# The first norm's product with the input: from GpSimd and ScalarE to one VectorE operation per tile

## The chip, the cores and the metric

The kernel runs on one core of a Trainium2 chip. The metric is the time of one execution on the device, in microseconds, as the median of several runs. TensorE multiplies matrices into PSUM, VectorE and ScalarE do the element-wise work, GpSimd does some of it, and SyncE only issues transfers. The profile calls them PE, DVE, ACT, POOL and SP.

## What is computed

A decoder block on 512 tokens of width 1024: an RMS norm modulated by a conditioning vector c, two attention mixers side by side, a gated merge, a second modulated norm and a squared-ReLU MLP. The part that the change touches is the first line of it:

```python
mod = c @ w_ada[layer] + b_ada[layer]
sh_a, sc_a, gt_a, sh_m, sc_m, gt_m = jnp.split(mod, 6, axis=-1)

h = modulate(rmsnorm(x, g_mix[layer]), sh_a, sc_a)   # rmsnorm(x, g) * (1 + sc_a) + sh_a
z = h @ w_in[layer]
```

## The kernel before

Activations lie transposed: x is eight tiles x0 to x7 of 128 channels by 512 tokens. A product in fp32 accuracy is made of three matmuls: every operand is split in a rounded part and the rest (hh and hl for h, w_hi and w_lo for a weight), and TensorE multiplies hh by w_hi, hh by w_lo and hl by w_hi.

**The start** (L76 to L269) is written in the order in which it runs; behind it a scheduler orders the instructions by its own model of their costs. ScalarE squares the tiles of x, VectorE adds the squares (L144), TensorE sums them over the channels, and some small operations (L157 to L165) give 1/rms of each token, rstd. Transposes with the identity (L168) spread it over all partitions into a PSUM tile, `rb`. The loop of L233 then goes through the eight tiles k of x:

- Modulation. `ada_dot` (L100) loads 128 columns of w_ada, 512 KB, and makes their dot products with c in one VectorE operation (L107), whose second output is a column of `mod`. Two such columns belong to a tile, scale and shift. L114 makes `a_k`, the tile's scale times the norm's gain, and L118 `shc`, its shift. The dots are spread: tile k's loop body makes the columns of tile k+1, one of them ahead of hl (L260) and one behind it (L263). The columns' buffers are five, so the transfer of one waits until the dot five before it has run. SyncE issues all loads in the order of the program.
- h. For tile 0, VectorE makes x0 times a_k times rstd in one operation that reads `rb` from PSUM (L248), ScalarE adds the shift and rounds into hh (L249), and VectorE makes hl as (x0 + shift) - hh (L251). ScalarE then copies rstd into SBUF, `rstd_sb` (L253). For tiles 1 to 7, GpSimd multiplies x_k by `rstd_sb` (L255), ScalarE makes hh from it with scale a_k and shift (L256), and then the same again into x_k without rounding (L258); VectorE subtracts (L261).
- The tile's weights, 448 KB, are rounded by ScalarE (L246), and VectorE makes the rest, w_lo (L250, L257).
- TensorE adds the tile's share to seven PSUM tiles at once (L267): seven matmuls hh by w_hi, seven hh by w_lo, seven hl by w_hi.

VectorE, ScalarE, GpSimd and TensorE each work through their own row of instructions in order, and wait for the others where they read what those make. Behind the loop the next weights are split (L183, L184) and multiplied (L197 to L199), and the seven tiles are evacuated from PSUM. Some microseconds later the first head's attention scores are formed (L547 to L555), read by VectorE (L344) and mixed on TensorE with the products of the second value unit.

Of the kernel before, what the change touches and what calls it, by code (L numbers as in the profile page):

```python
# [12 lines left out]
AF = mybir.ActivationFunctionType  # L13
ALU = mybir.AluOpType
# [5 lines left out]
KT = D // P  # L20
# [26 lines left out]
def block_kernel(ctx: ExitStack, tc: tile.TileContext, d):  # L47
    nc = tc.nc
# [17 lines left out]
    def tmp(name):  # L66
        return sb.tile([P, S], F32, name=name, tag="tmp", bufs=NB["tmp"])

    def f(ap):
        return ap.bitcast(F32)  # L70


    def wtile(shape=(P, 1024)):
        return sb.tile(list(shape), F32, name="w_raw", tag="w_raw", bufs=NB["raw"])
# [7 lines left out]
    xt = [big_x(f"x{k}") for k in range(KT)]  # L82
# [17 lines left out]
    def ada_dot(col, early=False):  # L100
        if early:
            w = sb.tile([P, 1280], F32, name="w_ada", tag="p", bufs=NB["p"])[:, 0:D]
        else:
            w = wtile()
        nc.sync.dma_start(w, d["w_ada"][col])
        junk = sb.tile([P, D], BF16, name="junk", tag="pT", bufs=NB["pT"])
        nc.vector.scalar_tensor_tensor(junk, w, 1.0, cb, op0=ALU.mult, op1=ALU.mult,  # L107
                                       accum_out=mod[:, col:col + 1])
# [3 lines left out]
    def scale_col(out, col, k, g):  # L112

        nc.vector.scalar_tensor_tensor(out[:, k:k + 1], mod[:, col:col + 1], badd[:, (k if g == C_GMIX else 8 + k):(k if g == C_GMIX else 8 + k) + 1],  # L114
                                       cols[:, g + k:g + k + 1], op0=ALU.add, op1=ALU.mult)

    def bias_col(col, n=1, scale=None):
        nc.vector.tensor_tensor(modb[:, col:col + n], mod[:, col:col + n],  # L118
                                cols[:, C_BADA + col:C_BADA + col + n], op=ALU.add)
# [107 lines left out]
    rb = st0.rstd("m", "o")  # L227
# [4 lines left out]
    NW = NG0 * P  # L232
    for k in range(KT):  # L233
        scale_col(amix, 2 * k, k, C_GMIX)
        if k == 0:
            ada_dot(1, True)
        bias_col(2 * k + 1)
        raw = wtile()
        nc.sync.dma_start(raw[:, :NW], d["w_g0"][k])
        a_k = amix[:, k:k + 1]  # L240
        shc = modb[:, 2 * k + 1:2 * k + 2]
        hh = big_a(f"hh{k}", F32R)
        hl = big_a(f"hl{k}", F32R)
        whi = sb.tile([P, 1024], F32R, name="w_hi", tag="w_hi", bufs=NB["hi"])
        wlo = sb.tile([P, 1024], F32R, name="w_lo", tag="w_lo", bufs=NB["lo"])
        nc.scalar.activation(whi[:, :NW], raw[:, :NW], AF.Copy)  # L246
        if k == 0:
            nc.vector.scalar_tensor_tensor(xt[k], xt[k], a_k, rb, op0=ALU.mult, op1=ALU.mult)  # L248
            nc.scalar.activation(hh, xt[k], AF.Identity, bias=shc)  # L249
            nc.vector.tensor_tensor(wlo[:, :NW], raw[:, :NW], f(whi[:, :NW]), op=ALU.subtract)  # L250
            nc.vector.scalar_tensor_tensor(hl, xt[k], shc, f(hh), op0=ALU.add, op1=ALU.subtract)  # L251
            rstd_b = tmp("rstd_sb")
            nc.scalar.activation(rstd_b, rb, AF.Copy)  # L253
        else:
            nc.gpsimd.tensor_tensor(xt[k], xt[k], rstd_b, op=ALU.mult)  # L255
            nc.scalar.activation(hh, xt[k], AF.Identity, bias=shc, scale=a_k)  # L256
            nc.vector.tensor_tensor(wlo[:, :NW], raw[:, :NW], f(whi[:, :NW]), op=ALU.subtract)  # L257
            nc.scalar.activation(xt[k], xt[k], AF.Identity, bias=shc, scale=a_k)  # L258
            if k < KT - 1:
                ada_dot(2 * k + 2, True)  # L260
            nc.vector.tensor_tensor(hl, xt[k], f(hh), op=ALU.subtract)  # L261
        for c in range(2 * k + 2 if k == 0 else 2 * k + 3, min(2 * k + 4, 2 * KT)):
            ada_dot(c, True)  # L263
        h.append((hh, hl))
        for w, v in ((whi, hh), (wlo, hh), (whi, hl)):
            for n in range(NG0):
                nc.tensor.matmul(g0_ps[n], w[:, n * P:(n + 1) * P], v, start=(k == 0 and w is whi and v is hh),  # L267
                                 stop=(k == KT - 1 and v is hl))
# [430 lines left out]
    for step in ORDER.split():  # L699
        op, a = step[0], int(step[1:] or 0)  # L700
# [48 lines left out]
    xt = [big_x(f"xr{k}") for k in range(KT)]  # L749
# [48 lines left out]
    for hf, tok in enumerate(HALVES):  # L798
# [4 lines left out]
        rb = st1.rstd("m", "o", tok)  # L803
        for k in range(KT):
            shc = modb[:, SCM + 2 * k + 1:SCM + 2 * k + 2]
            hh, hl = h2[k][0][:, tok], h2[k][1][:, tok]
# [208 lines left out]
    for hf, tok in enumerate(HALVES):  # L1015
# [6 lines left out]
        rb = st2.rstd("m", "o", tok)  # L1022
        k = 0
# [120 lines left out]
```

## Time and profile before

| | us |
|---|---|
| median of 3 runs | 822.92 (822.32 to 823.15) |
| the profiled execution | 820.9 |
| its span, first to last instruction | 819.1 |

| engine | busy us | share of the span |
|---|---|---|
| PE (matmul) | 796.0 | 97% |
| DVE | 608.7 | 74% |
| ACT | 393.0 | 48% |
| POOL | 141.1 | 17% |

The profile shows one execution, about 2 us under the median of the timed runs. An engine's busy time is a mean over the whole span; what an edit of one stage is worth is read in that stage, from the waits of the engine that sets its end. In the timeline a row holds the start in us, the duration in us, the engine, the line, the operation, what it writes and reads, its size, the count, and in brackets the idle time before it with what ended that. Operations of one engine overlap a little at their ends, so the distance from one start to the next is somewhat shorter than a duration.

### The profile page before, as it was taken

To read this page: it belongs to the slowest core of one execution; us is meant where nothing else is said; L and a number is where in the kernel's file an instruction comes from. 1 tells how busy PE (TensorE), PEld (TensorE's weight loads), DVE (VectorE), ACT (ScalarE), POOL (GpSimd) and SP (SyncE) were. 2 spreads that over 40 slices of the span, in tenths; PEclk is the share of its full clock that TensorE was granted. 3 is DMA by queue.
4 is the path that set the end of the run, shared out by engine and by line. 5 is a ranking of instruction groups with operands and counts; after the bars stand their busy time and mean duration, and the time that the engine had idled before them with its cause. 6 is when DMAs were issued, how large, how long until landed. Compare 5 with 4: busy or idle time off the path is not lost.

```text
span 819.1 us, 11898 instructions
## 1 busy us (share of the span) xinstructions
PE 796.0 (97%) x4444; PEld 645.2 (79%) x4444; DVE 608.7 (74%) x1179; ACT 393.0 (48%) x742; POOL 141.1 (17%) x123
## 2 busy tenths in 40 slices
PE   6899999999999999999999999999999999999896
PEld 3687668665577565888889998899899988998895
DVE  6978668887667788866677749886768776877854
ACT  5458526475334444332242446644574456445741
POOL 2500000000000000001300004450435043614200
PEclk8999999999999999999999999999999999999998
DMA  9683261010052034885247302333222422332203
GB/s 350 248 271 127 68 216 52 27 51 27 26 177 80 1 103 137 263 300 200 93 154 255 117 10 94 105 105 126 78 98 97 138 81 78 104 129 83 99 1 103
DMA packets 31005, 99.76 MB, mean 122 GB/s; under 512 B 3522, under 2 KB 5762, under 8 KB 30947
## 3 DMA queue, kind: packets, MB, share of 16 engines
q1 hardware_dynamic: 30880, 98.89, 35.9%
q8 instruction: 35, 0.57, 0.3%
q14 instruction: 24, 0.19, 0.1%
q0 software_dynamic: 64, 0.11, 0.0%
q10 hardware_dynamic: 2, 0.00, 0.0%
HBM read 96.89 MB, written 2.10 MB: 121 GB/s over the span
## 4 chain that ended last, share of the span: by engine, by line
PE 83%; DVE 7%; ACT 3%; DMA 2%; issue 2%; POOL 2%; SPq 0%; DVEq 0%; POOLq 0%; ACTq 0%
PE ps_acc L197 12%; PE ps_acc L199 12%; PE ps_acc L198 12%; PE ps_s L874 8%; PE ps_t L874 6%; PE ps_t L391 4%; PE ps_o L572 4%; PE ps_s L197 3%; PE ps_s L198 3%; PE ps_s L199 3%; PE ps_s L644 2%; PE ps_o L657 2%; POOL wsum L845 2%; DMA w_raw<-in_w_fc_dram 1%; DVE junk L107 1%
## 5 line engine op out<-in xcount | busy, mean ns | idle before, releaser
L183 ACT ACTIVATE w_hi<-w_raw 128x1024 fp32r<-128x1024 f32 x76 | 80.5, 1060 | 131.1 <-PE ps_acc L198 47.5
L184 DVE TENSOR_TENSOR w_lo<-w_raw,w_hi 128x1024 fp32r<-128x1024 f32 x76 | 99.5, 1311 | 54.4 <-ACT w_hi L183 54.2
L346 ACT ACTIVATE p<-p,nm 128x128 f32<-128x128 f32 (+3 forms) x96 | 53.3, 556 | 59.1 <-DVE nm L344 57.8
L199 PE MATMUL ps_acc<-hh,w_lo 128*128 128x512 f32 x200 | 80.1, 401 | 0.0
L198 PE MATMUL ps_acc<-hl,w_hi 128*128 128x512 f32 x200 | 79.8, 399 | 0.0
L197 PE MATMUL ps_acc<-hh,w_hi 128*128 128x512 f32 x200 | 79.7, 399 | 0.0
L379 DVE COPY pT<-ps_t 128x512 f32<-128x512 f32 (+1 forms) x72 | 42.4, 599 | 28.1 <-PE ps_o L572 15.8
L832 ACT ACTIVATE ws_hi<-wsum 128x512 fp32r<-128x512 f32 x56 | 35.3, 631 | 57.7 <-POOL wsum L845 55.0
L107 DVE SCALAR_TENSOR_TENSOR junk<-w_raw,cb 128x1024 bf16<-128x1024 f32 x32 | 38.5, 1220 | 17.9 <-DMA w_raw<-in_w_ada_dram 17.9
L845 POOL TENSOR_TENSOR wsum<-w_raw 128x512 f32<-128x512 f32 x28 | 39.2, 1399 | 65.1 <-DMA w_raw<-in_w_fc_dram 53.6
L845 POOL TENSOR_TENSOR wsum<-wsum,w_raw 128x512 f32<-128x512 f32 x28 | 45.9, 1640 | 25.2 <-DVE ws_lo L833 24.9
L198 PEld LDWEIGHTS ps_acc<-hl,w_hi 128*128 128x128 f32 x200 | 37.6, 188 | 10.8 <-issue 4.2
L197 PEld LDWEIGHTS ps_acc<-hh,w_hi 128*128 128x128 f32 x200 | 37.6, 188 | 10.8 <-issue 3.9
L199 PEld LDWEIGHTS ps_acc<-hh,w_lo 128*128 128x128 f32 x200 | 37.6, 188 | 10.5 <-issue 3.8
L833 DVE TENSOR_TENSOR ws_lo<-wsum,ws_hi 128x512 fp32r<-128x512 f32 x56 | 42.9, 796 | 3.1 <-PE ps_t L874 1.8
L197 PE MATMUL ps_acc<-h2h,w_hi 128*128 128x512 f32 x112 | 43.6, 389 | 0.0
L198 PE MATMUL ps_acc<-h2l,w_hi 128*128 128x512 f32 x112 | 43.6, 389 | 0.0
L199 PE MATMUL ps_acc<-h2h,w_lo 128*128 128x512 f32 x112 | 43.6, 389 | 0.0
L874 PE MATMUL ps_t<-t,ws_hi 128*128 128x256 f32 x224 | 40.5, 281 | 0.7 <-DVE t L962 0.4
L391 PEld LDWEIGHTS ps_t<-ident,p 128*128 128x128 f32 x240 | 27.6, 141 | 16.1 <-issue 5.4
L833 DVE TENSOR_TENSOR w_lo<-w_raw,w_hi 128x1024 fp32r<-128x1024 f32 (+1 forms) x28 | 31.1, 1111 | 10.2 <-ACT w_hi L832 10.2
L391 PE MATMUL ps_t<-ident,p 128*128 128x128 f32 x240 | 37.2, 279 | 0.0
(528 smaller groups left out, 2275.5 us busy)
## 6 DMA issues: line engine op xcount, KB each, us to landing
w_raw<-in_w_fc_dram SPq DMA_DIRECT2D x64, 512.0 KB, 3.3
w_raw<-in_w_ada_dram SPq DMA_DIRECT2D x32, 512.0 KB, 4.3
w_raw<-in_w_z_dram SPq DMA_DIRECT2D x25, 512.0 KB, 4.3
w_ada<-in_w_ada_dram SPq DMA_DIRECT2D x16, 512.0 KB, 6.5
w_raw<-in_w_c_dram SPq DMA_DIRECT2D x8, 512.0 KB, 4.2
w_raw<-in_w_o_dram SPq DMA_DIRECT2D x8, 512.0 KB, 4.6
w_raw<-in_w_out_dram SPq DMA_DIRECT2D x8, 512.0 KB, 3.2
w_raw<-in_w_g_dram SPq DMA_DIRECT2D x8, 448.0 KB, 7.0
```

The source lines that it names most:

```text
L107: nc.vector.scalar_tensor_tensor(junk, w, 1.0, cb, op0=ALU.mult, op1=ALU.mult, accum_out=mod[:, col:col + 1])
L183: nc.scalar.activation(hi[:, :n], raw[:, :n], AF.Copy)
L184: nc.vector.tensor_tensor(lo[:, :n], raw[:, :n], f(hi[:, :n]), op=ALU.subtract)
L197: nc.tensor.matmul(out, w[0], x[0], start=first, stop=False)
L198: nc.tensor.matmul(out, w[0], x[1], start=False, stop=False)
L199: nc.tensor.matmul(out, w[1], x[0], start=False, stop=last)
L346: nc.scalar.activation(o, o, AF.Exp, bias=nm, scale=-1.0, accum_out=sm)
L379: nc.vector.tensor_copy(dst, src)
L391: nc.tensor.transpose(pp[:, off:off + P], aps[i][:, kb * P:(kb + 1) * P], ident)
L833: nc.vector.tensor_tensor(lo, src, f(hi), op=ALU.subtract)
L845: nc.gpsimd.tensor_tensor(t, sums[x_] if isinstance(x_, int) else x_, y_, op=ALU.add)
L874: nc.tensor.matmul(out, w[a_][:, k], x[k][b_], start=(first and k == 0 and j == 0), stop=(k == 3 and j == 2), skip_group_check=True)
```

## The change

Tiles 1 to 7 get what tile 0 has. VectorE makes x_k times a_k times rstd in one operation that reads `rb` from PSUM, ScalarE makes hh with the shift as its bias, and VectorE makes hl from x_k, the shift and hh in one operation. GpSimd's products, ScalarE's second pass over x_k and the copy `rstd_sb` are gone. The dots stay spread as they were, and SyncE's transfers keep their order in the start.

```diff
         nc.scalar.activation(whi[:, :NW], raw[:, :NW], AF.Copy)
-        if k == 0:
-            nc.vector.scalar_tensor_tensor(xt[k], xt[k], a_k, rb, op0=ALU.mult, op1=ALU.mult)
-            nc.scalar.activation(hh, xt[k], AF.Identity, bias=shc)
-            nc.vector.tensor_tensor(wlo[:, :NW], raw[:, :NW], f(whi[:, :NW]), op=ALU.subtract)
-            nc.vector.scalar_tensor_tensor(hl, xt[k], shc, f(hh), op0=ALU.add, op1=ALU.subtract)
-            rstd_b = tmp("rstd_sb")
-            nc.scalar.activation(rstd_b, rb, AF.Copy)
-        else:
-            nc.gpsimd.tensor_tensor(xt[k], xt[k], rstd_b, op=ALU.mult)
-            nc.scalar.activation(hh, xt[k], AF.Identity, bias=shc, scale=a_k)
-            nc.vector.tensor_tensor(wlo[:, :NW], raw[:, :NW], f(whi[:, :NW]), op=ALU.subtract)
-            nc.scalar.activation(xt[k], xt[k], AF.Identity, bias=shc, scale=a_k)
-            if k < KT - 1:
-                ada_dot(2 * k + 2, True)
-            nc.vector.tensor_tensor(hl, xt[k], f(hh), op=ALU.subtract)
+        nc.vector.scalar_tensor_tensor(xt[k], xt[k], a_k, rb, op0=ALU.mult, op1=ALU.mult)
+        nc.scalar.activation(hh, xt[k], AF.Identity, bias=shc)
+        nc.vector.tensor_tensor(wlo[:, :NW], raw[:, :NW], f(whi[:, :NW]), op=ALU.subtract)
+        if 0 < k < KT - 1:
+            ada_dot(2 * k + 2, True)
+        nc.vector.scalar_tensor_tensor(hl, xt[k], shc, f(hh), op0=ALU.add, op1=ALU.subtract)
         for c in range(2 * k + 2 if k == 0 else 2 * k + 3, min(2 * k + 4, 2 * KT)):
             ada_dot(c, True)
```

In the new code the product stands in L247, hh in L248, w_lo in L249 and hl in L252; all lines behind the loop are nine lower.

VectorE's row in tile 1 (x_68 is x1; hh_213, hl_214 and hh_211, hl_212 are hh1 and hl1 before and after; junk is the dot's unused first output), as a piece of the difference:

```order
 L118 TENSOR_TENSOR modb<-mod,cols 128x1
-L257 TENSOR_TENSOR w_lo<-w_raw,w_hi 128x896
-L107 SCALAR_TENSOR_TENSOR junk,mod<-w_ada,cb 128x1024
-L261 TENSOR_TENSOR hl_214<-x_68,hh_213 128x512
+L247 SCALAR_TENSOR_TENSOR x_68<-x_68,amix,ps_o 128x512
+L249 TENSOR_TENSOR w_lo<-w_raw,w_hi 128x896
+L107 SCALAR_TENSOR_TENSOR junk,mod<-w_ada,cb 128x1024
+L252 SCALAR_TENSOR_TENSOR hl_212<-x_68,modb,hh_211 128x512
 L107 SCALAR_TENSOR_TENSOR junk,mod<-w_ada,cb 128x1024
 L114 SCALAR_TENSOR_TENSOR amix<-mod,badd,cols 128x1
```

One operation more per tile, in front of w_lo, and hl in the three-operand form; the dots and everything else keep their places.

TensorE's row some 10 us behind the loop, before (kh_509 and kl_511 are the keys' two parts, qst the query, zv the first value unit, hh_169, hh_213 and hh_256 are hh0, hh1 and hh2):

```order
L316 MATMUL ps_m<-ident,zg 128x32 x4
L197 MATMUL ps_acc<-hh_169,w_hi 128x512
L198 MATMUL ps_acc<-hl_170,w_hi 128x512
L199 MATMUL ps_acc<-hh_169,w_lo 128x512
L197 MATMUL ps_acc<-hh_213,w_hi 128x512
L554 MATMUL ps_s<-kh_509,qst 128x384
L555 MATMUL ps_s<-kl_511,qst 128x384
L198 MATMUL ps_acc<-hl_214,w_hi 128x512
L199 MATMUL ps_acc<-hh_213,w_lo 128x512
```

The same place now (kh_500, kl_502 the keys, hh_211 and hl_212 are hh1 and hl1):

```order
L197 MATMUL ps_acc<-hh_169,w_hi 128x512
L198 MATMUL ps_acc<-hl_170,w_hi 128x512
L307 MATMUL ps_m<-ident,zg 128x32 x4
L199 MATMUL ps_acc<-hh_169,w_lo 128x512
L197 MATMUL ps_acc<-hh_211,w_hi 128x512
L198 MATMUL ps_acc<-hl_212,w_hi 128x512
L199 MATMUL ps_acc<-hh_211,w_lo 128x512
L545 MATMUL ps_s<-kh_500,qst 128x384
L546 MATMUL ps_s<-kl_502,qst 128x384
```

The small transposes of the gates stand two matmuls later and the scores of 384 keys two matmuls later. The following 40 or so matmuls differ in the same manner, and VectorE's and ScalarE's rows there by the operations that belong to these scores; from the end of that stretch on the rows are the same again.

## Rows read from the trace of the kernel before

**Rows 1.** Waits of PE, 17 to 92 us: engine, line, waited-for: us, times, longest.

```profile
PE ps_acc L267 <- DVE hl L261: 1.5, 1, 1.5
PE ps_acc L267 <- ACT hh L256: 1.4, 1, 1.4
```

**Rows 2.** Busy time by stretch: us, PE, PEld, DVE, ACT, POOL, clock, DMA.

```profile
13.00:16.80 3.80, 1.11 (x4) 0.71 (x4) 3.52 (x11) 1.73 (x4) 0.00 (x0) 0.50 1.03 412
...
24.50:33.00 8.50, 5.52 (x24) 3.92 (x23) 8.50 (x10) 2.51 (x4) 6.75 (x9) 1.00 0.46 155
33.00:61.60 28.60, 28.60 (x127) 23.66 (x128) 23.53 (x43) 16.43 (x21) 0.00 (x0) 1.00 0.85 281
...
72.00:92.00 20.00, 19.54 (x90) 14.49 (x90) 18.75 (x65) 15.46 (x44) 0.00 (x0) 1.00 0.13 47
```

**Rows 3.** Timeline of PE, 24 to 62 us: first matmuls of tiles, waits, L197.

```profile
24.63 0.62 PE L267 MATMUL ps_acc<-hh,w_hi 128*128 128x512 f32 x2
...
29.51 0.74 PE L267 MATMUL ps_acc<-hl,w_hi 128*128 128x512 f32 x2 [1.54 <-DVE hl L261]
...
32.86 0.73 PE L267 MATMUL ps_acc<-hh,w_hi 128*128 128x512 f32 x2 [1.44 <-ACT hh L256]
...
37.75 0.61 PE L267 MATMUL ps_acc<-hh,w_hi 128*128 128x512 f32 x2
...
61.55 0.39 PE L197 MATMUL ps_acc<-hh,w_hi 128*128 128x512 f32 x1
```

**Rows 4.** Timeline of DVE, 15 to 36 us.

```profile
15.36 0.74 DVE L248 SCALAR_TENSOR_TENSOR x<-x,amix,ps_o 128x512 f32<-128x512 f32 x1
16.02 1.08 DVE L250 TENSOR_TENSOR w_lo<-w_raw,w_hi 128x896 fp32r<-128x896 f32 x1
17.02 0.75 DVE L251 SCALAR_TENSOR_TENSOR hl<-x,modb,hh 128x512 fp32r<-128x512 f32 x1
17.68 2.31 DVE L107 SCALAR_TENSOR_TENSOR junk<-w_ada,cb 128x1024 bf16<-128x1024 f32 x1
...
22.14 1.23 DVE L114 SCALAR_TENSOR_TENSOR amix<-mod,badd,cols 128x1 f32<-128x1 f32 x1
...
23.36 2.19 DVE L257 TENSOR_TENSOR w_lo<-w_raw,w_hi 128x896 fp32r<-128x896 f32 x1
...
27.72 1.74 DVE L261 TENSOR_TENSOR hl<-x,hh 128x512 fp32r<-128x512 f32 x1
...
31.62 0.21 DVE L114 SCALAR_TENSOR_TENSOR amix<-mod,badd,cols 128x1 f32<-128x1 f32 x1
...
31.82 1.08 DVE L257 TENSOR_TENSOR w_lo<-w_raw,w_hi 128x896 fp32r<-128x896 f32 x1
32.82 1.22 DVE L107 SCALAR_TENSOR_TENSOR junk<-w_ada,cb 128x1024 bf16<-128x1024 f32 x1
...
33.96 0.69 DVE L261 TENSOR_TENSOR hl<-x,hh 128x512 fp32r<-128x512 f32 x1
34.57 1.22 DVE L107 SCALAR_TENSOR_TENSOR junk<-w_ada,cb 128x1024 bf16<-128x1024 f32 x1
...
35.71 0.22 DVE L114 SCALAR_TENSOR_TENSOR amix<-mod,badd,cols 128x1 f32<-128x1 f32 x1
```

**Rows 5.** Timeline of POOL, its products merged.

```profile
17.43 13.18 POOL L255 TENSOR_TENSOR x<-x,rstd_sb 128x512 f32<-128x512 f32 x7 [14.77 <-ACT rstd_sb L253]
```

**Rows 6.** Timeline of ACT: hh of tile 0 and of tile 2.

```profile
16.14 0.72 ACT L249 ACTIVATE hh<-x,modb 128x512 fp32r<-128x512 f32 x1 [2.07 <-DVE x L248]
...
31.99 0.81 ACT L256 ACTIVATE hh<-x,modb,amix 128x512 fp32r<-128x512 f32 x1 [5.95 <-DVE modb L118]
```

**Rows 7.** DVE groups by shape, 340 to 480 us: count, busy, mean ns, idle.

```profile
L765 DVE SCALAR_TENSOR_TENSOR yb<-tab,ps_s 128x512 f32<-128x512 f32 x8 | 5.5, 688 | 5.5 <-PE ps_s L199 5.5
```

**Rows 8.** Instructions on the tile w_ada: its transfers from issue to landing.

```profile
DMA to landing us min/median/max: 3.2/6.5/9.3
```

**Rows 9.** Timeline of DVE, 60 to 96 us: a group of scalings.

```profile
82.56 1.01 DVE L369 TENSOR_SCALAR p<-p,rc 128x128 f32<-128x128 f32 x3
```

## The prediction

> **What bounds the kernel now.** TensorE is busy 97% of the span, so I read its waits first. Behind its first matmuls two of them lie in the loop that the change edits, the first modulation and projection (L233 to L268): one for hl1, which L261 makes on VectorE, and one for hh2, which L256 makes on ScalarE [rows 1]. The stretches by time say the same: of 24.5 to 33.0 us TensorE is busy 5.52 of 8.50 us, and from 33.0 to 61.6 it has no idle time at all, at a granted clock of 1.00 in both [rows 2]. So what an edit of this loop is worth is what it takes from those two waits, and nothing else, as long as the operands of the later tiles still come in time.
>
> TensorE's starts give the exact size. Tile 1's first matmul starts at 24.63 us, right behind tile 0's last, tile 2's at 32.86, tile 3's at 37.75, and the first matmul behind the loop (L197) at 61.55 [rows 3]. Tiles 3 to 7 follow each other without a wait, so one tile costs (61.55 - 37.75) / 5 = 4.76 us. Seven tiles would be 33.32 us; from 24.63 to 61.55 are 36.92. The difference, **3.60 us**, is what both waits cost with the slow first matmuls behind them.
>
> Why the operands are late stands in VectorE's row of instructions. Up to 17.4 us its operations have their usual lengths: 0.74 for the product x0 with PSUM (L248), 1.08 for w_lo. From 17.68 on a dot takes 2.31 (four of them do), the one-column amix 1.23, w_lo 2.19, hl1 1.74; from 31.62 on the same forms take 1.22, 0.21, 1.08 and 0.69 [rows 4]. That is 4 + 1 + 1 + 1 = 7 operations, each longer by 1.0 to 1.1 us, and it is the stretch in which GpSimd makes its seven products x times rstd, 17.43 to 30.61 us [rows 5]. VectorE has no idle time there (8.50 of 8.50 in one of the stretches), so about 7 x 1.07 = 7.5 us of its queue are lost beside GpSimd.
>
> **The change part by part.** *Removed:* GpSimd's seven products (L255), ScalarE's copy of rstd and its seven second passes over x (L253, L258). ScalarE waits for VectorE's modb in front of the hh of these tiles, by 5.95 us for hh2 [rows 6]; its passes lie beside such waits and are worth nothing by themselves. Without GpSimd's products I take VectorE's operations of 17.68 to 31.62 at the lengths that they have outside.
>
> *Added on VectorE, per tile 1 to 7:* one product of x with a_k and rstd in PSUM (L247), and hl as a three-operand form (L252) in place of a subtraction. Both forms stand in tile 0: from start to start x0 takes 16.02 - 15.36 = 0.66 and hl0 17.68 - 17.02 = 0.66, where the subtraction takes 34.57 - 33.96 = 0.61 [rows 4]. Tile 0's product ran while TensorE did little (1.11 of 3.80 us [rows 2]); the price of a read of PSUM beside running matmuls is shown by the same form on 512 columns in L765, 0.688 us long, eight times [rows 7]. So it is no dearer there, and I keep 0.66. The period of a tile on VectorE was 35.71 - 31.62 = 4.09 us and becomes 4.09 + 0.66 + 0.05 = 4.80, and with about 0.03 for a product that starts only when amix is through, **4.83 us**, 0.07 above TensorE's 4.76. VectorE is now the slower of the two, and what covers that is its lead.
>
> *The lead.* hl0 starts at 17.02 as before and the first dot at 17.68. Two dots at 1.14 from start to start (33.96 - 32.82) [rows 4] end at 19.96; amix and modb take 31.82 - 31.62 = 0.20, so L247 for x1 starts at 20.16 and ends at 20.90. ScalarE's hh takes 0.72 with bias alone [rows 6], so hh1 is there at about 21.7, before TensorE wants it at 24.63. w_lo1 ends near 21.9. The dot and then hl1 follow: hl1 runs from 22.96 to 23.7; TensorE wants it after 14 of the tile's 21 matmuls, at 24.63 + 3.17 = 27.80. The wait for hl1 is gone. x2 starts at 20.16 + 4.83 = 24.99, hh2 is there at 26.5 and is wanted at 24.63 + 4.76 = 29.39: the wait for hh2 is gone with 2.9 us to spare. Each later tile eats 0.07, so hh7 (50.7 against 53.19) still has some 2.5 us. TensorE is late on nothing in the loop, and the loop ends at 61.55 - 3.60 = 57.95.
>
> *What else could be late next.* The dots now run earlier and ask for their columns of w_ada earlier. A transfer is issued when the dot five before it has freed its buffer; the shortest such time is that of tile 3's second dot, whose buffer is free when tile 1's first dot ends (22.96) and which runs at 33.3, 10.3 us later; the slowest transfer of these columns took 9.3 to land [rows 8]. Covered, by a microsecond at the least. GpSimd's small memsets move to the start of its row, where the other engines wait for x, and a configuration step in front of its first product moves to the y stage, where the product's result is not the next thing that TensorE reads; I take nothing for either. Behind the loop all operands of the next products (w_hi, w_lo, the evacuations) are released by the same loop's matmuls or by hl7 and move with it.
>
> *Moved by the scheduler.* Behind the loop the order of TensorE's row changes in one place, some 11 us after the loop's end: the score matmuls of the first head and the products of the second value unit interleave a matmul or two later or earlier (the TensorE rows in the section on the change). The work is the same. TensorE loses 0.46 of 20.00 us there now, and VectorE, which must read each score before its PSUM buffer is used again, is busy 18.75 of 20.00 [rows 2]. So the new order can win at most 0.46 and could lose something that the trace does not show. I take 0 and put 0.4 of gain and 1.0 of loss in the range, the loss as a little more than the longest operation that could newly stand ahead of a score there, a 1.01 us group of scalings that now precedes one [rows 9].
>
> **Sum.** -3.60 us on the path, 0 for the rest. The profiled execution took 820.9 us (span 819.1), so it would become 817.3. It stands 2.0 us under the median of the three runs, 822.92; I take the same difference off the median: **819.3 us**, -0.44%.
>
> [...] Tile 0's hl0 is the form that all tiles now get, with two fp32 sources in SBUF: 0.75 us against 0.69 for the subtraction [rows 4]. [...]
>
> **The rivals.**
> 1. *The gain is spent again in the new order behind the loop.* For it: VectorE is 94% busy there, and the order was laid out by a scheduler's own model. Against it: TensorE's loss there is small with almost the same order, and later stages have no wait that is tied to an absolute time. To bring the time within 0.2% of before (1.65 us; about what a measurement of this kernel can tell from no change) it must lose 2 us or more, two scores late by a microsecond each. Time: about 821.9, from 821.3 to 822.9.
> 2. *VectorE's long operations are not GpSimd's doing*, but come from the transfers, which are dense in that stretch too. Then the seven operations stay long and two products are added in front of hh2: it comes 2 x 0.68 later plus the wait for the product and its pass on ScalarE, near 34.8 instead of 32.8. TensorE then follows VectorE at 4.83 per tile: 34.8 + 5 x 4.83 + 4.76 = 63.7 instead of 61.55, **+2.2 us, 825.1**, slower. It decides as soon as hh7 comes later than 56.79, which is a period of 5.84 on VectorE from x1 at 20.16 on. Against it: from 13.0 to 16.8 us the transfers run at 412 GB/s and VectorE's operations have their short lengths, and from 24.5 to 33.0 they move only 155 GB/s and the operations are long [rows 2, 4].
> [...]
>
> **How the numbers follow.** The forecast, within about a microsecond of 819.3: 0.77. Rival 1: 0.12. Rival 2: 0.05. Rival 3: 0.03; the rest, 0.03, goes to costs that no row points at. Faster by over 0.2% are the forecast, rival 3 and 0.01 of the rest: 0.81. Same: rival 1 and 0.01: 0.13. Slower: rival 2 and 0.01: 0.06. The range: 0.4 us of gain and 1.0 of loss from the moved order, and the spread of the three runs (822.32 to 823.15) on either side, 818.0 to 821.1; to take in rival 3 with its spread and the lower edge of rival 1, it goes to 821.6. That leaves out most of rival 1 and rival 2, somewhat under 2 in 10.
>
> **What would show it.** In the changed kernel's trace: no wait of TensorE for hl or hh between 17 and 58 us; the first L197 about 3.6 us earlier, near 57.95; all sixteen dots near 1.22 us and w_lo near 1.08; L247 and L252 near 0.74; a tile's period on VectorE near 4.83; GpSimd without products before the y stage; and TensorE's idle time in the 20 us of scores behind the loop still under a microsecond. [...]

## The result and the profile after

| | median us | runs |
|---|---|---|
| before | 823.15 | 5 (822.32 to 824.96) |
| the changed kernel | **818.24** | 5 (817.83 to 819.28) |

The ratio is 0.9948, 95% interval 0.9936 to 0.9959: 4.3 us less, with 3.4 and 5.3 as its ends; the two medians of the table differ by 4.91. The forecast was 819.3, faster. The profiled execution took 819.3 us, its span is 817.5.

The waits of TensorE from 17 to 92 us, where [rows 1] had one for hl1 and one for hh2 (columns: engine, what it makes, line, what it waited for; us in all, times, longest):

```profile
PE ps_acc L258 <- ACT hh L248: 1.7, 1, 1.7
PE ps_m L299 <- PE ps_acc L197: 0.4, 1, 0.4
PE ps_m L307 <- DVE krs L301: 0.3, 1, 0.3
```

What is left in the loop is the wait for hh0, ahead of the very first matmul, which the kernel before has too (1.7). The stretches by time (us, then busy time of PE, PEld, DVE, ACT, POOL, clock, DMA), which answer to [rows 2]; the last one is the stretch of the first scores, which before lay from 72 to 92:

```profile
24.50:33.00 8.50, 8.50 (x39) 7.03 (x38) 8.50 (x17) 2.92 (x4) 0.00 (x0) 1.00 0.95 322
33.00:57.60 24.60, 24.60 (x110) 20.38 (x109) 22.21 (x39) 8.79 (x13) 0.00 (x0) 1.00 0.78 256
68.40:88.40 20.00, 19.43 (x89) 14.70 (x90) 18.68 (x65) 15.42 (x44) 0.00 (x0) 1.00 0.11 43
```

TensorE is busy 8.50 of 8.50 us where it was busy 5.52. In the scores it loses 0.57 instead of 0.46. The starts of tiles 0, 1, 2 and 7 and of the first L197, which answer to [rows 3]:

```profile
17.81 1.22 PE L258 MATMUL ps_acc<-hh,w_hi 128*128 128x512 f32 x2 [1.74 <-ACT hh L248]
...
24.30 0.62 PE L258 MATMUL ps_acc<-hh,w_hi 128*128 128x512 f32 x2
...
29.06 0.62 PE L258 MATMUL ps_acc<-hh,w_hi 128*128 128x512 f32 x2
...
52.86 0.62 PE L258 MATMUL ps_acc<-hh,w_hi 128*128 128x512 f32 x2
...
57.62 0.39 PE L197 MATMUL ps_acc<-hh,w_hi 128*128 128x512 f32 x1
```

From 24.30 to 57.62 are 33.32 us, seven times 4.76 to the hundredth; before it was 36.92. VectorE from 17 to 58 us by shape (count, busy us, mean ns, idle), which answers to [rows 4]:

```profile
L107 DVE SCALAR_TENSOR_TENSOR junk<-w_ada,cb 128x1024 bf16<-128x1024 f32 x14 | 17.0, 1218 | 0.0
L249 DVE TENSOR_TENSOR w_lo<-w_raw,w_hi 128x896 fp32r<-128x896 f32 x8 | 8.7, 1084 | 0.0
L252 DVE SCALAR_TENSOR_TENSOR hl<-x,modb,hh 128x512 fp32r<-128x512 f32 x8 | 6.0, 747 | 0.0
L247 DVE SCALAR_TENSOR_TENSOR x<-x,amix,ps_o 128x512 f32<-128x512 f32 x8 | 6.0, 746 | 0.0
```

No long dot is left (1.22 each), and both three-operand forms take 0.75. The period of a tile, from one amix to the next (20.88, 25.75, and so on to 50.09), with the last hh, hh7, on ScalarE in the second fence:

```profile
20.88 0.21 DVE L114 SCALAR_TENSOR_TENSOR amix<-mod,badd,cols 128x1 f32<-128x1 f32 x1
...
21.13 0.75 DVE L247 SCALAR_TENSOR_TENSOR x<-x,amix,ps_o 128x512 f32<-128x512 f32 x1
...
25.75 0.21 DVE L114 SCALAR_TENSOR_TENSOR amix<-mod,badd,cols 128x1 f32<-128x1 f32 x1
```

```profile
51.12 0.72 ACT L248 ACTIVATE hh<-x,modb 128x512 fp32r<-128x512 f32 x1 [3.30 <-DVE x L247]
```

That is 4.87 us per tile, and hh7 is ready at 51.84, 1.0 us before TensorE takes it at 52.86.

### The profile page after: what moved, and what is told of

Same layout as the page of the kernel before. It is cut to its first block, busy times and chain, and to the rows that moved or that the text cites. A ratio compares the mean times of both kernels' runs of the same rounds, so it can differ in the third digit from the quotient of the medians.

```text
span 817.5 us, 11881 instructions
## 1 busy us (share of the span) xinstructions
PE 795.0 (97%) x4444; PEld 645.4 (79%) x4444; DVE 605.3 (74%) x1186; ACT 385.7 (47%) x734; POOL 127.1 (16%) x116
## 4 chain that ended last, share of the span: by engine, by line
PE 81%; DVE 5%; DMA 5%; ACT 4%; issue 3%; POOL 2%; SPq 0%; DVEq 0%; POOLq 0%; ACTq 0%
PE ps_acc L197 10%; PE ps_acc L199 10%; PE ps_acc L198 10%; PE ps_s L865 8%; PE ps_t L865 7%; PE ps_t L382 4%; PE ps_o L563 4%; DMA w_raw<-in_w_fc_dram 3%; PE ps_s L197 2%; PE ps_s L198 2%; PE ps_s L199 2%; PE ps_s L635 2%; PE ps_o L648 2%; POOL wsum L836 1%; PE ps_acc L258 1%
## 5 line engine op out<-in xcount | busy, mean ns | idle before, releaser
L183 ACT ACTIVATE w_hi<-w_raw 128x1024 fp32r<-128x1024 f32 x76 | 80.3, 1059 | 129.0 <-PE ps_acc L198 47.9
L199 PE MATMUL ps_acc<-hh,w_lo 128*128 128x512 f32 x200 | 80.2, 401 | 0.0
L197 PE MATMUL ps_acc<-hh,w_hi 128*128 128x512 f32 x200 | 79.6, 398 | 0.0
L197 PEld LDWEIGHTS ps_acc<-hh,w_hi 128*128 128x128 f32 x200 | 37.6, 188 | 10.8 <-issue 3.9
L199 PEld LDWEIGHTS ps_acc<-hh,w_lo 128*128 128x128 f32 x200 | 37.6, 188 | 10.4 <-issue 3.8
L197 PE MATMUL ps_acc<-h2h,w_hi 128*128 128x512 f32 x112 | 43.6, 389 | 0.0
L199 PE MATMUL ps_acc<-h2h,w_lo 128*128 128x512 f32 x112 | 43.6, 389 | 0.0
```

What stands on the lines that cost most here:

```text
L183: nc.scalar.activation(hi[:, :n], raw[:, :n], AF.Copy)
L197: nc.tensor.matmul(out, w[0], x[0], start=first, stop=False)
L199: nc.tensor.matmul(out, w[1], x[0], start=False, stop=last)
```

## The experiments

The theory: VectorE's long operations were GpSimd's doing, in that both read SBUF; the gain is TensorE's two waits. The rivals: the transfers made them long; or the gain comes from the shorter code on GpSimd and ScalarE and not from VectorE's lengths. Every run stands beside runs of the kernel before on the same chip, and the expectations call the runs by number: e1 to e4 (e1_again, e2_pool_reads, e3_pool_memsets, e4_no_product) share a median of 822.56 us, e5 to e8 (e5_extra_product, e6_two_tiles, e7_warm, e8_pool_copies) 822.12, and e9 to e12 (e9_again, e10_warm, e11_before_warm, e12_half_products) 822.51. Below they stand in the order of the argument: e1, e2, e3, e8, e4, e6, e5, e7 and e9 to e12.

### The changed kernel again

> The changed kernel itself, once more, to see how much of the first result (4.9 us less by the medians) is the loop. Theory A (the loop's two waits, 3.6 us, and nothing else): 3 to 4 us less than the kernel before in the same rounds; the loop itself, from the first matmul of tile 1 to the first L197, takes 7 x 4.76 = 33.3 us, as in the first profile. Rival B (the changed order behind the loop, or something later, gains too): 4.5 us or more less, and in the profile the distance from the first L197 to the last matmul shorter than the 750.7 us of the kernel before.

818.20 us, ratio 0.9947 [0.9933, 0.9961]. The loop's ends in its profile:

```profile
24.06 0.62 PE L258 MATMUL ps_acc<-hh,w_hi 128*128 128x512 f32 x2
...
57.38 0.39 PE L197 MATMUL ps_acc<-hh,w_hi 128*128 128x512 f32 x1
```

Again 33.32 us. The 4.4 us by the time lie between theory A's 3 to 4 and rival B's 4.5 or more; rival B's other sign fails, for from the start of the first L197 to that of the last matmul are 751.6 us here (57.38 to 809.00) and 750.5 before (61.55 to 812.02). The result stands, and 0.8 us of it are not placed.

### GpSimd's reads put back, for nothing

```diff
+        if k == 0:
+            rstd_b, dm = tmp("rstd_sb"), tmp("dm")
+            nc.scalar.activation(rstd_b, rb, AF.Copy)
+        else:
+            nc.gpsimd.tensor_tensor(dm, rstd_b, rstd_b, op=ALU.mult)
```

> The changed kernel with seven products on GpSimd beside the loop again, of a copy of rstd with itself into a scratch tile that nothing reads, released at the same point as the old ones; what is computed is the same. Theory G (GpSimd's reading of SBUF holds VectorE up): seven VectorE operations of some 18 to 32 us are again 1.0 to 1.1 us longer, VectorE's queue is 7.5 us late, hh7 comes near 59 instead of 52 us, the loop ends about 6 us later than in the changed kernel, and the time is some 5.5 to 6.5 us above it, 1 to 2 us above the kernel before. Rival T (the transfers made the operations long, and GpSimd was only there at the same time): all VectorE operations keep their lengths and the time is that of the changed kernel.

822.51 us, ratio 1.0001 [0.9991, 1.0012]: the whole gain is gone, though nobody reads what GpSimd makes. VectorE's timeline beside these products:

```profile
18.89 2.06 DVE L107 SCALAR_TENSOR_TENSOR junk<-w_ada,cb 128x1024 bf16<-128x1024 f32 x1
...
22.86 0.98 DVE L114 SCALAR_TENSOR_TENSOR amix<-mod,badd,cols 128x1 f32<-128x1 f32 x1
23.77 0.15 DVE L118 TENSOR_TENSOR modb<-mod,cols 128x1 f32<-128x1 f32 x1
23.96 0.75 DVE L247 SCALAR_TENSOR_TENSOR x<-x,amix,ps_o 128x512 f32<-128x512 f32 x1
...
27.81 1.51 DVE L252 SCALAR_TENSOR_TENSOR hl<-x,modb,hh 128x512 fp32r<-128x512 f32 x1
```

Four dots of 2.05 to 2.06, the amix, one w_lo (1.27) and the hl are longer, by 5.1 us in all. The product of L247, which has one of its two tensor inputs in PSUM, keeps its 0.75 in the same stretch. So does modb its 0.15, although both its inputs are in SBUF; it stands right behind the amix. TensorE waits again, and once VectorE's lead is used up it follows VectorE's 4.87 per tile (33.04, 37.93, 42.81 in its starts):

```profile
25.52 0.74 PE L263 MATMUL ps_acc<-hh,w_hi 128*128 128x512 f32 x2 [0.41 <-ACT hh L248]
...
33.04 0.73 PE L263 MATMUL ps_acc<-hh,w_hi 128*128 128x512 f32 x2 [1.77 <-ACT hh L248]
```

I had expected 5.5 to 6.5 us of loss. It was 4.3, since a hold is at most 0.84 here and not 1.07 (5.1 us in all where I had put 7.5); the last experiment says why.

### GpSimd busy, but only writing

```diff
+        if k == 0:
+            rstd_b = tmp("rstd_sb")
+            nc.scalar.activation(rstd_b, rb, AF.Copy)
+        else:
+            for _ in range(4):
+                nc.gpsimd.memset(rstd_b, 0.0)
```

> The changed kernel with 28 memsets of 128x512 on GpSimd beside the loop, into the scratch copy of rstd: GpSimd writes SBUF for some 14 us from the same point on, but reads nothing; what is computed is the same. If VectorE is held up by GpSimd's reads alone: VectorE's operations keep 1.22, 1.08 and 0.74 us, time as the changed kernel. If any GpSimd access to SBUF holds it up: operations longer by up to half a microsecond each (a memset's length, 0.52), VectorE's period of 4.87 us per tile rises above 5.5 in that stretch, and the time goes up by 1 to 6 us.

817.59 us, ratio 0.9941 [0.9927, 0.9955]: no loss, with GpSimd busy in the same place for longer than its products were. GpSimd's timeline with all 28 memsets merged, and VectorE's dots by shape:

```profile
18.28 16.32 POOL L258 MEMSET rstd_sb<- 128x512 f32 x28 [15.63 <-ACT rstd_sb L255]
```

```profile
L107 DVE SCALAR_TENSOR_TENSOR junk<-w_ada,cb 128x1024 bf16<-128x1024 f32 x14 | 17.0, 1219 | 0.0
```

So it isn't that GpSimd works there, or writes SBUF there: a dot takes 1.22 beside the memsets and 2.06 beside the products of e2_pool_reads, which read SBUF. It is its reads.

### One input only

```diff
+        if k == 0:
+            rstd_b, dm = tmp("rstd_sb"), tmp("dm")
+            nc.scalar.activation(rstd_b, rb, AF.Copy)
+        else:
+            nc.gpsimd.tensor_copy(dm, rstd_b)
+            nc.gpsimd.tensor_copy(dm, rstd_b)
```

> The changed kernel with fourteen copies of rstd's tile into a scratch tile on GpSimd beside the loop (one input in SBUF each, where the old products had two); what is computed is the same. If any read of SBUF by GpSimd holds up VectorE's operations with two SBUF inputs: up to fourteen of them longer, each by about one copy's length (0.6 us or so), VectorE some 5 to 8 us late after them, time 3 to 5 us above the changed kernel. If only GpSimd's operations with two inputs do: lengths and time as in the changed kernel, 818.2.

821.87 us, ratio 0.9997 [0.9987, 1.0006]. A copy reads one tensor and takes 0.62 alone, and it holds VectorE up as well: dots of 1.63, an amix of 0.55, while L247 stays at 0.75:

```profile
18.71 1.63 DVE L107 SCALAR_TENSOR_TENSOR junk<-w_ada,cb 128x1024 bf16<-128x1024 f32 x1
...
21.82 0.55 DVE L114 SCALAR_TENSOR_TENSOR amix<-mod,badd,cols 128x1 f32<-128x1 f32 x1
...
22.48 0.75 DVE L247 SCALAR_TENSOR_TENSOR x<-x,amix,ps_o 128x512 f32<-128x512 f32 x1
```

Six dots, three amix, one w_lo and two hl are long, by 4.6 us together; two waits for hh take the gain back.

### The kernel before without GpSimd's products

```diff
         else:
-            nc.gpsimd.tensor_tensor(xt[k], xt[k], rstd_b, op=ALU.mult)
             nc.scalar.activation(hh, xt[k], AF.Identity, bias=shc, scale=a_k)
```

> The kernel before without GpSimd's seven products: x of tiles 1 to 7 is left without its factor rstd, everything else runs as before (ScalarE's two passes, the subtraction for hl). Theory G: the whole gain of the change is GpSimd's absence, so VectorE's operations are short, both waits of TensorE in the loop are gone, and the time is that of the changed kernel within 0.5 us. Rival C (the gain comes from the shorter chain: one VectorE product in place of GpSimd's product and a ScalarE pass): hh1 and hh2 still late, time within 1 us of the kernel before.

818.54 us, ratio 0.9946 [0.9932, 0.9959]: the gain of the change, with ScalarE's two passes and VectorE's subtraction as they were before. Its loop:

```profile
24.57 0.63 PE L266 MATMUL ps_acc<-hh,w_hi 128*128 128x512 f32 x2
...
57.90 0.39 PE L197 MATMUL ps_acc<-hh,w_hi 128*128 128x512 f32 x1
```

33.33 us, and VectorE's fourteen dots have a mean of 1218 ns. This kernel also leaves out hh's wait for GpSimd's products; the run with the reads put back had no such wait and lost the gain all the same, so the wait is not the cause. What the change wins is that GpSimd is out; VectorE's added work costs nothing, and ScalarE's saved passes bring nothing.

### Two tiles in the new form

L247, L248 and L252 for tiles 1 and 2, the old form behind them, which leaves GpSimd five products:

```diff
+        if k < 3:
+            nc.vector.scalar_tensor_tensor(xt[k], xt[k], a_k, rb, op0=ALU.mult, op1=ALU.mult)
...
+        else:
+            nc.gpsimd.tensor_tensor(xt[k], xt[k], rstd_b, op=ALU.mult)
```

> The kernel before with the new form in tiles 1 and 2 alone; tiles 3 to 7 keep GpSimd's product and ScalarE's second pass. GpSimd then makes five products beside tiles 0 to 2 instead of seven. Theory G: five VectorE operations between 17 and 28 us are 1.0 to 1.1 us longer, VectorE is some 5.3 us late when it makes x2, hh2 comes near 32 instead of 29.4 us, and TensorE loses about 2.6 of the 3.6 us again: time 821 to 822. Rival C (the late operands came from the long chain over GpSimd and ScalarE, and the first two tiles were the late ones): both waits gone, time as the changed kernel, 818.2.

820.77 us, ratio 0.9984 [0.9975, 0.9994], a little under the 821 to 822 of theory G. GpSimd's products end at 26.92, and VectorE's next operation with two SBUF inputs has its short length:

```profile
17.64 9.28 POOL L258 TENSOR_TENSOR x<-x,rstd_sb 128x512 f32<-128x512 f32 x5 [14.98 <-ACT rstd_sb L256]
```

```profile
25.69 2.32 DVE L107 SCALAR_TENSOR_TENSOR junk<-w_ada,cb 128x1024 bf16<-128x1024 f32 x1
...
27.93 0.74 DVE L253 SCALAR_TENSOR_TENSOR hl<-x,modb,hh 128x512 fp32r<-128x512 f32 x1
```

TensorE waits for hh1 and hh2, though both now come in the new form:

```profile
25.27 0.72 PE L270 MATMUL ps_acc<-hh,w_hi 128*128 128x512 f32 x2 [1.60 <-ACT hh L249]
...
31.54 0.72 PE L270 MATMUL ps_acc<-hh,w_hi 128*128 128x512 f32 x2 [0.93 <-ACT hh L249]
```

So rival C, the long chain, falls. TensorE's seven tiles take 34.98 (25.27 to 60.25), so 1.66 of the 3.60 us are lost again; I had put it at 2.6.

### A second product on VectorE

```diff
+        if k == 1:
+            dm = tmp("dm")
+        if k > 0:
+            nc.vector.scalar_tensor_tensor(dm, xt[k], a_k, rb, op0=ALU.mult, op1=ALU.mult)
         nc.vector.scalar_tensor_tensor(xt[k], xt[k], a_k, rb, op0=ALU.mult, op1=ALU.mult)
```

> The changed kernel with the product of tiles 1 to 7 made twice on VectorE, the first time into a scratch tile that nothing reads (0.66 us more per tile); what is computed is the same. It prices VectorE's lead. From the changed kernel's rows: hh1 0.66 later, near 23.35 us, then hh of tile k at 23.35 + 5.53 (k - 1); TensorE wants it at 24.30 + 4.76 (k - 1). Theory L (VectorE is 0.11 us per tile slower than TensorE now and lives on a lead of about 1.6 us at tile 1): TensorE waits some 0.8 us in front of each tile from tile 3 on, the loop ends 3.4 to 3.7 us later, time 821.5 to 822. Rival (VectorE has room to spare beside TensorE): no waits, time as the changed kernel, 818.2.

824.05 us, ratio 1.0021 [1.0008, 1.0033], some 2 us above what I expected. VectorE's period is 5.65 (4.87 and 0.78, since the second product starts 0.78 behind the first), and TensorE follows it, tile by tile, as soon as the lead is gone. The last tile brings 1.2 us more. TensorE's starts of tiles 4, 6 and 7 and of L197, then ScalarE at the last tile:

```profile
40.44 0.73 PE L262 MATMUL ps_acc<-hh,w_hi 128*128 128x512 f32 x2 [0.56 <-ACT hh L252]
...
51.75 0.74 PE L262 MATMUL ps_acc<-hh,w_hi 128*128 128x512 f32 x2 [0.60 <-ACT hh L252]
...
58.60 0.73 PE L262 MATMUL ps_acc<-hh,w_hi 128*128 128x512 f32 x2 [1.76 <-ACT hh L252]
...
63.50 0.39 PE L197 MATMUL ps_acc<-hh,w_hi 128*128 128x512 f32 x1
```

```profile
56.88 1.06 ACT L183 ACTIVATE w_hi<-w_raw 128x1024 fp32r<-128x1024 f32 x1 [3.40 <-PE ps_m L262]
57.84 0.71 ACT L252 ACTIVATE hh<-x,modb 128x512 fp32r<-128x512 f32 x1
```

x7 was ready at 56.59, but ScalarE had a rounding of the next stage's weights (L183) in front of hh7, which itself waited for TensorE's tile 6. In the changed kernel hh7 comes first. So a tile of 4.87 on VectorE is covered by the lead and one of 5.65 isn't. Even without L183 in front, hh7 would have come near 57.3, behind the 56.79 that the prediction's second rival gave as the point from which it is slower than before.

### More idle matmuls ahead of the loop

TensorE waits for rstd at a granted clock of 0.50 (13.0 to 16.8 us in the kernel before [rows 2]), and tile 0 begins at it: pairs of 1.05 to 1.22 us, where later ones take 0.62. Two more of the idle matmuls that keep it busy, and four between the sums and the loop:

```diff
-WARM = (0, 2)
+WARM = (0, 2, 4, 5)
...
-    rb = st0.rstd("m", "o")
+    rb = st0.rstd("m", "o", between=lambda: nc.tensor.matmul(warm, ones, xt[6], start=True, stop=True))
+    for _ in range(3):
+        nc.tensor.matmul(warm[:, 0:256], ones, xt[7][:, 0:256], start=True, stop=True)
```

> The changed kernel with more idle matmuls on TensorE ahead of the loop: two more tiles of x behind the two that are there, one between the sums of the squares and the transposes of rstd, three half ones behind the transposes, all into a PSUM tile that nothing reads; what is computed is the same. In the changed kernel's profile the granted clock is still 0.50 when tile 0 starts at 17.81 and 1.00 from 21.24 on, and tile 0 takes 6.5 us where the other tiles take 4.76. If TensorE's work ahead of the loop keeps the clock at 1.00: tile 0 takes near 4.8 us, TensorE wants hh2 earlier than VectorE has it and then follows VectorE at 4.87 us per tile, in all 1.0 to 2.0 us less than the changed kernel, 816.2 to 817.2. If not: the time of the changed kernel, or up to 1 us more where the idle matmuls stand in front of the sums or the transposes.

**815.80 us**, ratio 0.9922 [0.9900, 0.9943], the fastest median of all and 0.4 under what was expected. The changed kernel had not run on that chip, so the last set holds it too, e9_again:

> The changed kernel once more, beside the three that follow. All theories: 4.0 to 4.9 us under before (ratio 0.994 to 0.995), first L197 between 57.3 and 58.2 us, seven tiles in 33.32.

817.02 us, ratio 0.9935 [0.9920, 0.9951]; its loop again takes 33.33 us, from 25.20 to 58.53. The seven tiles came out as expected, the rest didn't: the time is 5.3 us under before (5.5 by the medians) and not 4.0 to 4.9, and the loop ends 0.3 later than the 58.2 given. Then the idle matmuls once more, e10_warm:

> The changed kernel with more idle matmuls ahead of the loop, as in e7_warm, now beside the changed kernel itself. e7_warm was some 2 us faster by its time, but its loop ended only 0.1 to 0.9 us earlier than in the profiles of the changed kernel. Theory A: the idle matmuls are worth what the loop's end shows, 0.2 to 0.9 us against e9_again. Theory B: they are worth the 2 us of the time, and some of it stands behind the loop.

816.03 us, ratio 0.9926 [0.9910, 0.9943], 1.0 us under the changed kernel beside it (0.7 by the ratios); the two intervals overlap, so that it is faster isn't shown. TensorE's starts of tiles 0, 1 and 2 and of the first matmul behind the loop (L199 here):

```profile
17.39 0.73 PE L262 MATMUL ps_acc<-hh,w_hi 128*128 128x512 f32 x2 [0.91 <-ACT hh L252]
...
22.28 0.70 PE L262 MATMUL ps_acc<-hh,w_hi 128*128 128x512 f32 x2
...
27.16 0.71 PE L262 MATMUL ps_acc<-hh,w_hi 128*128 128x512 f32 x2
...
56.35 0.39 PE L199 MATMUL ps_acc<-hh,w_hi 128*128 128x512 f32 x1
```

Tile 0 now takes 4.89 us where it took 6.2 to 7.4. The lead is spent by that, and TensorE follows VectorE at 4.87 per tile (34.07 for seven instead of 33.32). The loop ends at 56.35 and, in e7_warm's profile, at 57.27, a mean of 56.8 against 57.8 for the three profiles of the changed kernel (57.62, 57.38, 58.53). That is of the size of the 1.0 us of the times, which is nearer to theory A than to theory B; but the ends scatter by 0.9 and 1.2 us within either kernel, so neither is shown, nor what made the 2 us between the first two sets. The same matmuls in the kernel before, e11_before_warm:

> The kernel before with the same idle matmuls, GpSimd's products left in. Theory A: hl1 and hh2 come when VectorE makes them, as before, so a shorter tile 0 on TensorE only makes it wait longer: the waits grow by what tile 0 loses, the first L197 stays within 0.9 us of 61.55, and the time stays within 1 us of before. Theory B: 2 us faster than before, as e7_warm was against the change.

821.18 us, ratio 0.9987 [0.9976, 0.9998]. Its waits in the loop:

```profile
PE ps_acc L271 <- ACT hh L260: 3.8, 2, 2.4
PE ps_acc L271 <- DVE hl L265: 1.6, 1, 1.6
PE ps_acc L271 <- ACT hh L253: 0.9, 1, 0.9
```

A new wait of 2.4 for hh1 stands in front of the two old ones, and the first L199 starts at 61.69, where L197 stood at 61.55. Before the change TensorE only waits longer behind a quicker tile 0, as theory A says of the loop. The time is 1.1 us under before by the ratio and 1.3 by the medians, a little more than theory A's 1 us, and this gain is not in the loop and, from this run, not placed. So the 1.0 us in the changed kernel can't be put down to the loop with certainty either.

### Half products

```diff
-            nc.gpsimd.tensor_tensor(xt[k], xt[k], rstd_b, op=ALU.mult)
+            for a in (0, 256):
+                nc.gpsimd.tensor_tensor(xt[k][:, a:a + 256], xt[k][:, a:a + 256], rstd_b[:, a:a + 256], op=ALU.mult)
```

> The kernel before with each of GpSimd's products made in two halves of 256 columns. In the runs so far a VectorE operation with two SBUF inputs was longer by the shortest time of the GpSimd operation beside it less 0.2 us: 1.09 by products of 1.29, 0.84 by products of 1.04, 0.41 by copies of 0.62. Theory: it waits for one GpSimd operation each time. A half product should take some 0.65 to 0.7 alone, so a dot takes 1.22 + 0.45 to 0.5 = 1.67 to 1.72 and the one-column amix about 0.65 to 0.7; up to 14 operations are held up, 5 to 7 us in all, and the time is within 2 us of before, rather under it. Rival: each held operation loses about 1.07 whatever GpSimd's operation is; then dots stay at 2.3, more of them are long, and the time is 3 us or more over before.

820.98 us, ratio 0.9981 [0.9971, 0.9991]. GpSimd's instructions of that line (shortest, median and longest ns), then VectorE's timeline:

```profile
L256 POOL TENSOR_TENSOR x<-x,rstd_sb x14: 720/1588/1719, 17.9 to 35.6; 128x256 f32<-128x256 f32 x14
```

```profile
18.18 1.76 DVE L107 SCALAR_TENSOR_TENSOR junk<-w_ada,cb 128x1024 bf16<-128x1024 f32 x1
...
21.55 0.68 DVE L114 SCALAR_TENSOR_TENSOR amix<-mod,badd,cols 128x1 f32<-128x1 f32 x1
...
25.47 1.22 DVE L262 TENSOR_TENSOR hl<-x,hh 128x512 fp32r<-128x512 f32 x1
```

A dot is longer by 0.54, an hl by 0.53: the shortest product (0.72) less 0.2, as the theory says, and half of what it was by the whole products. Fourteen operations are held where there were seven, and the time is within 2 us of before, as expected. The fixed loss of 1.07 is out.

## Why the prediction was right

**The bound and its size.** Right. The loop gave up its two waits and no other came: 36.92 became 33.32, the 3.60 us of the sum, in the profiles of the changed kernel, of the memsets and of the kernel without products (33.32 to 33.33). The time gave more: 4.3 [3.4, 5.3] and 4.4 [3.2, 5.5] us in two sets, which take in 3.60, and 5.3 [4.0, 6.6] in the third, which doesn't. So about 1 us of the gain by the times may lie outside the sum. It doesn't show behind the loop: from the first L197 to the span's end are 757.6 us before and 759.9, 758.6 and 759.2 in the three profiles of the changed kernel, which is more, and one program's executions differ there by over a microsecond (over all fourteen profiles, in either form, it is 756.4 to 759.9). Where that last microsecond stands is open. It nearly took the time out of the forecast: 818.24 is 1.06 under 819.3 and close to the range's lower end. Without the 0.4 us that the range allowed for a gain in the moved order, where nothing was gained, the end would have been some 818.5, above the time. That part is luck.

**VectorE's lengths.** Right, and the point on which all of it hung. Rival 2 (the transfers) falls: in the changed kernel they move 322 GB/s where the long operations had 155 [rows 2], and the dots are short (1.22); with GpSimd's reads put back, the dots are long (2.06). Two things kept their lengths in the experiments: L247, with one input in PSUM, 0.75 beside the reads of e2_pool_reads and e8_pool_copies, and the dots, 1.22 beside the 28 memsets of e3_pool_memsets.

**The added work.** Right in price: L247 0.75 and L252 0.75 in all tiles. Rival 3, a dearer hl, to which the prediction gives 0.03 and which its range takes in, is shown by no run: the eight L252 took 0.747 on average, where L247 with one input in PSUM takes 0.746. The period was 4.87 and not 4.83: from amix to L247 pass 0.25 us, not 0.23, and the operations behind it add a hundredth here and there.

**The lead.** Right that it suffices, but it was mis-sized: hh7 had 1.0 us to spare, not 2.5. VectorE's row started 0.9 later (hl0 at 17.93 against 17.02), tile 1 began 0.33 earlier on TensorE, and six periods took 0.04 more each. In the changed kernel's first profile the late start comes from the sum of the squares, eight matmuls of one column ahead of rstd. They take 1.86 us:

```profile
11.86 1.86 PE L154 MATMUL ps_m<-ones,sq 128*128 128x1 f32 x8 [2.02 <-DVE sq L144]
```

In before they take 1.05, from 11.76, and the clock falls to 0.50 behind them [rows 2]. The column shows 1.00 ahead of the loop in the changed kernel's profile, but tile 0's first pair of matmuls takes 1.22 there, as it does at 0.50 in the kernel before, and the trace's first record of the clock is its rise to 1.00 at 21.24; so I take the clock to have been low through these sums, an estimate from the lengths, as is the 0.50 in the expectation of e7_warm. It was so in the profiles of this execution, of e9_again and four experiments in the new form; in e1_again the eight take 1.05, but start at 12.68, so that tile 0 starts no earlier there (17.83). In the three profiles of the kernel before and of e4 and e6, which keep GpSimd's or ScalarE's old form in most tiles, they take 1.05. Six of seven against none of three may mean that the change has a part in it; no run isolates that. It moves little: tile 0 starts later and then lasts from 6.2 to 7.4 us instead of 7.7, tile 1 starts at 24.1 to 25.2 against 24.6, and so the loop's end lies between 57.4 and 58.5 (57.95 was forecast).

**Transfers and moved order.** Right. VectorE has no idle time ahead of a dot in the loop. The scores lose 0.11 us more than before, nothing that a measurement finds; rival 1 falls.

**The step from the span to the median.** The 2.0 us that the profiled execution stood under its median were carried over. The changed kernel's profiled execution stands 1.0 above its own. Only the difference of two medians had to hold: 3.60 us were forecast, and it was 4.3 by the ratio and 4.91 by the medians.

## What to carry to other kernels

When VectorE's operations change their length from one stretch to the next, look at what GpSimd reads there: a GpSimd operation that looks free in its own row can be paid for on VectorE, at most one hold per operation here (seven for seven products, twelve for fourteen copies), and a one-column operation can pay nearly as much as a large one (1.02 us for amix, 1.09 for a dot). The operation with an operand in PSUM was not held (L247, 0.75 beside the products and the copies; no run has that operand in SBUF), and the added VectorE time was free here since the lost time had been larger. An engine a little slower than the one it feeds (4.87 against 4.76) is covered by its lead, so count the lead in us for the last tile; speeding up the consumer at the start, as the idle matmuls did, uses that lead up.

## What the runs showed of the hardware

Beside the products the starts of the two engines' long operations alternated: GpSimd's at 17.43, 18.87 and 21.09 in the kernel before, VectorE's at 17.68, 19.92 and 22.14. A VectorE operation with two or more SBUF inputs and none in PSUM was longer by GpSimd's shortest time for its operation less 0.2 to 0.3 us, for 1024 columns and for one column alike. It was held less where GpSimd was already at work when it came, as the w_lo behind L247 (by 0.19 in e2_pool_reads, 0.30 in e6_two_tiles), and not at all where it came between two copies (the w_lo at 29.97 in e8_pool_copies, 1.08; the copies run from 29.32 to 29.94 and from 30.00 on). One form was never held: modb, two inputs of one column right behind amix, 0.14 to 0.15 us with and without GpSimd's reads; no run says why. The dots, 1.22 alone:

| GpSimd's operation | its shortest us | dot us | dot longer by |
|---|---|---|---|
| product of two tensors, 512 columns | 1.29 | 2.31 | 1.09 |
| product of a tensor with itself | 1.04 | 2.06 | 0.84 |
| product of two tensors, 256 columns | 0.72 | 1.76 | 0.54 |
| copy | 0.62 | 1.63 | 0.41 |
| memset | 0.53 | 1.22 | 0 |

GpSimd's instructions (shortest, median and longest ns), the products of the kernel before and the copies:

```profile
L255 POOL TENSOR_TENSOR x<-x,rstd_sb x7: 1290/2135/2255, 17.4 to 28.9; 128x512 f32<-128x512 f32 x7
```

```profile
L257 POOL COPY dm<-rstd_sb x7: 620/1488/1527, 18.4 to 33.1; 128x512 f32<-128x512 f32 x7
```

The one-column amix, 0.21 alone, took 1.23 beside the products. GpSimd's operations grew too: its products from 1.29 to as much as 2.25, its copies from 0.62 to as much as 1.53. Halving GpSimd's operations halved each hold here (a dot's from 1.09 to 0.54) and doubled their number, from 7 to 14.
